# One layer with 32 experts on one core: expert groups in another order, the order of the experts computed sooner, the surplus loop moved up

## The chip, the cores and the metric

The kernel runs on one core of a Trainium2 chip. The time is the device time in microseconds (us) of one execution; less is better. Three executions of the kernel before took 603.98, 604.2 and 605.28 us, with a median of 604.2 us.

## What is computed

The reference is one layer on 256 tokens of width 1024: a norm, an input projection, a gated recurrent part beside a differential attention, an output projection with a residual, and then a mixture of 32 experts, of which each token uses two. The change touches the mixture of experts and the last norm:

```python
h2 = rmsnorm(x, norm2_g[l])
x = x + hier_moe(h2, ...)          # router, then the loop below
for e in range(N_EXPERTS):         # 32 experts, 1024 -> 512 -> 1024
    hid = jax.nn.silu(t @ w_eg[e]) * (t @ w_eu[e])
    out = out + gates[:, e:e + 1] * (hid @ w_ed[e])
return rmsnorm(x, normf_g)
```

Each expert has three float32 matrices of 2 MB, gate, up and down. All 32 are read from HBM, 201 MB in all.

## The kernel before

The first 145 us are the part ahead of the experts (projections, attention, recurrence, router). The experts follow in groups. A **pair** is two experts with room for 64 tokens each, a **four** is four experts with room for 32 tokens each, so that every group fills the 128 rows of a tile. Experts 0 to 3 are the two fixed pairs. The other 28 are sorted at run time by how many tokens they have: the fullest eight go into four pairs, the other twenty into five fours. The list `groups` has the two fixed pairs, then the four sorted pairs, then the five fours.

One group goes through these steps: one-hot matrices (`one_hot`, L838) gather its tokens (`gather`, products at L799, scaled on VectorE at L800); the gate and up products run in `up` (L877), with Silu on ScalarE in between (`gate`, L884); `hidden` multiplies (L812), transposes (L816) and copies (L819); `down` multiplies by the down matrices (L894); and `scatter` adds the result to the four sums `acc` (L832), after `halves` has split it in two parts (L825, L826). The main loop emits the preparation of group g+1 between the up and the down products of group g. A product of a pair fills half of TensorE's columns, one of a four a quarter, so two or four of them run side by side; one step in the inner dimension takes a pair or a four equally long.

The weights come through a ring of 23 buffers of 1 MB, `order`, each filled by one DMA that SyncE (SP) issues at L767. A pair needs 12 of them, a four 24. SP works in order: for each load it waits until TensorE has freed the buffer, and until the load eight places earlier on one of eight DMA semaphores (`DMAHW0` to `DMAHW7`) has landed. For the sorted experts SP first reads their numbers out of the tile `permi` (L858).

`by_load` makes the sorted order with small products and VectorE operations: a count (L918, L920), a rank (L931) and the sorted list (L936), which VectorE casts into `permi` (L937). It is a generator, and the code that calls it sets after which products each part may stand (`issue_after`). The scheduler fills in the rest.

Tokens that don't fit into their expert's room are done in a loop behind a condition on the count `nov` (`tc.If`, `tc.For_i`, L1020 and L1021). In the executions shown it is skipped. Where it is skipped, SP still has to add to the DMA semaphores what the loop's six loads would have added; it does this at the end of its own branch, one semaphore after the other, and waits before each one until all earlier loads of that semaphore have landed.

At the end (L1002 onwards) the last four's gate and up products run, then `hidden`, eight products that spread the last norm's gain over all rows (L1012, from the 4 KB that ScalarE loads at L1007), the surplus loop, four products that keep the clock up (`keep_warm(NW5, ...)`, L186), the last down products (L894), the last sums (L1094), and the norm with the stores. The buffers `nfb`, `hT_l`, `zt`, `jk` and the loop's `wx_free` are ring buffers that are asked for with `free(i)`, each a different one.

Of the kernel before, what the change touches and what calls it, by code (L numbers as in the profile page):

```python
# [29 lines left out]
FF = 512  # L30
CAP = 64
# [6 lines left out]
NWA, NWB, NWZ = 6, 11, 6  # L38
NPJ = 4
NST = 4  # L40
NWARM, NW1, NW2, NW3, NW5 = 9, 2, 10, 4, 4
NL = 3


# [3 lines left out]
B_TRI, B_ONE, B_IG, B_WR, B_RB, B_NF, B_N = 176, 304, 432, 464, 784, 824, 952  # L48

N_FIX, N_PAIRED = 4, 12  # L50
# [54 lines left out]
def kernel(ctx: ExitStack, tc: tile.TileContext,  # L105
                       x, w_in, w_out, w_eg, w_eu, w_ed, pack_a, pack_b, pack_m, out, dbg=None):
# [632 lines left out]
    def pmm():  # L739
        return psm.tile([P, 512], F32, name="pmm", tag="pmm", bufs=4)  # L740
# [4 lines left out]
    wzs.append(ctx.enter_context(tc.tile_pool(name="wzl", bufs=1, side="right", reuse_waits="tile")))  # L745
    order = [wa] + wbs[:7] + [wa] + wbs[7:9] + [wa] + wbs[9:] + [wa] + wzs[:2] + [wa] * 2 + wzs[2:]
    count, loaded = [0], [None]
    groups = [range(j, j + 2) for j in range(0, N_PAIRED, 2)] + [range(j, j + 4) for j in range(N_PAIRED, NE, 4)]
    LAST = len(groups) - 1

    def load_w(src, rows, hf, pieces):

# [38 lines left out]
    def gather(n, G_, xg=None, per=4, ks=range(KD)):  # L791

        if xg is None:
            xg = mp.tile([P, KD, P], F32, name="xg", tag="xg", bufs=1)
        for k0 in ks[::per]:
            px_ = pmm()
            for i in range(per):
                for t in range(NT):
                    T.matmul(px_[:, i * P:i * P + n], x1c[:, t, k0 + i], G_[:, t], start=(t == 0), stop=(t == NT - 1))  # L799
            V.tensor_tensor(xg[:, k0:k0 + per, :n], px_.rearrange("p (k s) -> p k s", k=4)[:, :per, :n],  # L800
                            cb[:, B_N2 + k0:B_N2 + k0 + per, None].to_broadcast([P, per, n]), op=OP.mult)
        return xg

    def free(i):

        w = order[(count[0] + i) % len(order)].tile([P, 4, 512], F32, name="w", tag="w")
        return w.rearrange("p a b -> p (a b)")

    def hidden(n, sg_, pu_, gs, to=None):
        hid = mp.tile([P, 512], F32R, name="oH", tag="oH", bufs=1).bitcast(F32).rearrange("p (k s) -> p k s", k=4)  # L810

        V.scalar_tensor_tensor(hid[:n], sg_[:n].rearrange("p (q k) -> p k q", k=4), gs[:n, :1],  # L812
                               pu_[:n].rearrange("p (q k) -> p k q", k=4), op0=OP.mult, op1=OP.mult)
        pt = pmm()
        for k in range(4):
            T.transpose(pt[:, k * P:k * P + n], hid[:n, k], ident[:n, :n])  # L816
        hT = mp.tile([P, 512], F32R, name="oL", tag="oL", bufs=1).bitcast(F32) if to is None else to
        hT = hT.rearrange("p (k s) -> p k s", k=4)
        A.copy(hT[:, :, :n], pt.rearrange("p (k s) -> p k s", k=4)[:, :, :n])  # L819
        return hT  # L820
# [21 lines left out]
    def prep(g):  # L842

        js = groups[g]
        Gm = one_hot(js).rearrange("p t e c -> p t (e c)")
        if js[0] < N_FIX:
            r = rw[:, :, g]
        elif js[0] < N_PAIRED:
            r = rw2[:, :, g - N_FIX // 2]
        else:  # L850
            r = rw4[:, :, g - N_PAIRED // 2]
        return gather(P, Gm), *slots(P, Gm, r)

    def load(g):
# [14 lines left out]
    def up(ws, n_, xg, p_=None, ks=range(KD)):  # L869
        if p_ is None:  # L870
            p_ = pgu()
        n = len(ws) // 6
        cap = P // n
        for k in ks:
            for i in range(n):
                k4 = k % 4
                up_end[0] = T.matmul(p_[i * cap:(i + 1) * cap], xg[:, k, i * cap:(i + 1) * cap],  # L877
                         ws[n_, i, k // 4][:, k4 * FF:(k4 + 1) * FF], start=(k == 0), stop=(k == KD - 1))
        return p_

    def gate(ws, xg, rs, sg_=None, p_=None):
        if sg_ is None:
            sg_ = mp.tile([P, FF], F32R, name="oL", tag="oL", bufs=1).bitcast(F32)
        A.activation(sg_, up(ws, "g", xg) if p_ is None else p_, AF.Silu, scale=rs[:, :1])  # L884
        return sg_

    def down(ws, hT, ojs):
        n = len(ws) // 6
        cap = P // n
        for k in range(4):  # L890
            for j in range(2):
                for i in range(n):
                    c0 = (k % 2) * D + j * 512
                    T.matmul(ojs[j][i * cap:(i + 1) * cap], hT[:, k, i * cap:(i + 1) * cap],  # L894
                             ws["d", i, k // 2][:, c0:c0 + 512], start=(k == 0), stop=(k == 3))
        return ojs
# [14 lines left out]
    def by_load():  # L911

        E2 = 2 * NE
        km, kc = cb[:NE, B_KM:B_KM + NE], cb[:NE, B_KC:B_KC + NE]
        kmc, kcc, ec, half = (cb[:E2, B_KC + NE + i:B_KC + NE + i + 1] for i in range(4))
        pc = pmm()
        for t in range(NT):
            T.matmul(pc[:NE, :NE], warm[:, :NE], oh[:, t], start=(t == 0), stop=(t == NT - 1))  # L918
        for t in range(NT):
            T.matmul(pc[:NE, NE:NE + 1], oh[:, t], warm[:, 0:1], start=(t == 0), stop=(t == NT - 1))  # L920
        yield
        room = mp.tile([P, 512], F32R, name="oH", tag="oH", bufs=1).bitcast(F32)[:E2]
        key, kcol, pos = room[:NE, :NE], room[:NE, NE:NE + 1], room[:, NE + 1:NE + 2]
        bef, Pe = room[:NE, E2:E2 + NE].bitcast(BF16).rearrange("p (a e) -> p a e", a=2), room[:NE, 2 * E2:2 * E2 + NE // 2].bitcast(BF16)
        V.tensor_scalar(kcol, pc[:NE, NE:NE + 1], kmc[:NE], kcc[:NE], op0=OP.mult, op1=OP.add)
        V.tensor_tensor(key, pc[:NE, :NE], km, op=OP.mult)
        V.tensor_tensor(key, key, kc, op=OP.add)

        V.tensor_scalar(bef, key[:, None, :].to_broadcast([NE, 2, NE]), kcol, None, op0=OP.is_lt)
        V.tensor_copy(cnt, pc[:NE, NE:NE + 1])  # L930
        T.matmul(pc[:E2, E2:E2 + 1], bef.rearrange("p a e -> p (a e)"), warm[:NE, 0:1], start=True, stop=True)  # L931
        yield
        V.tensor_tensor(pos, pc[:E2, E2:E2 + 1], half, op=OP.add)
        V.tensor_scalar(Pm, iota[:E2, :E2], pos, None, op0=OP.is_equal)
# [43 lines left out]
    next(positions)  # L978
    p_0 = {"g": up(ws, "g", xg, None, range(4))}
    with tc.issue_after(up_end[0].ins):  # L980
        next(positions)
        p_0["u"] = up(ws, "u", xg, None, range(4))
    with tc.issue_after(up_end[0].ins):
        next(positions)
        gather(P, Gm, xg, 2, range(4, KD))
    for n_ in "gu":
        up(ws, n_, xg, p_0[n_], range(4, KD))
# [11 lines left out]
            scatter(P, S_, oj, j)  # L999
        ws = ws_n  # L1000
    xg_l, S_l, gs_l, rs_l = pre
    sg_l = gate(ws, xg_l, rs_l, free(0)[:, :FF])  # L1002
    hT_l = free(1)[:, :512]

    nfb = free(2)
    nfr = nfb[:KD, D:D + P]
    A.dma_start(nfr, pack_b[:KD, B_NF:])  # L1007
    hT_l = hidden(P, sg_l, up(ws, "u", xg_l), gs_l, hT_l)
    for j in range(2):
        p_ = pmm()  # L1010
        for k in range(4):
            T.matmul(p_[:, k * P:(k + 1) * P], ident[:KD, 4 * j + k:4 * j + k + 1].to_broadcast([KD, P]),  # L1012
                     nfr, start=True, stop=True)
        A.copy(nfb[:, j * 512:(j + 1) * 512], p_)
    tc.keep_in_program_order(A.preload_act_table_set(SET_EXP_LN))
    wx_free = [free(i) for i in range(3, 10)]
    zt, jk = free(10), free(11)

    n_ov = nc.values_load(nov[0:1, 0:1], min_val=0, max_val=2 * S // (CAP // 2 + 1))
    with tc.If(n_ov > 0):  # L1020
        with tc.For_i(0, n_ov, 1):  # L1021
# [31 lines left out]
                    SY.dma_start(wx[n_, hf], v[:, hf * 2048:(hf + 1) * 2048])  # L1053
            Gm = mp.tile([P, NT, 2, CAP], F32, name="Gm", tag="Gm", bufs=1)[:, :, 0]
            V.tensor_tensor(Gm, iota[:, None, :].to_broadcast([P, NT, CAP]), cr.to_broadcast([P, NT, CAP]), op=OP.is_equal)
            xg = gather(CAP, Gm, wx_free[6][:, :KD * P].rearrange("p (k s) -> p k s", k=KD))
            S_, gs, rs = slots(CAP, Gm, cw)
            pg_, pu_ = pgu(), pgu()
            for n_, p_ in (("g", pg_), ("u", pu_)):
# [18 lines left out]
                scatter(CAP, S_, oj, j)  # L1078


    ss = mp.tile([P, NT, 2], F32, name="ss")
    zt = [zt[:, t * D:(t + 1) * D] for t in range(NT)]
    oj = [pgu(), pgu()]
    keep_warm(NW5, oj[1])
    down(ws, hT_l, oj)
    oH = [jk[:, j * 512:(j + 1) * 512].bitcast(F32R) for j in range(2)]
    oL = [jk[:, (2 + j) * 512:(3 + j) * 512].bitcast(F32R) for j in range(2)]
    for j in range(2):
# [72 lines left out]
```

## Time and profile before

| | |
|---|---|
| median of three executions | 604.2 us |
| profiled execution: its time, its span | 603.43 us, 601.7 us |
| TensorE busy | 534.5 us (89%) |
| loads of the experts' weights | 1024 KB each, some of the last in halves and quarters |
| moved by DMA | 223.77 MB, 372 GB/s over the span |
| chain that ended last | PE 60%, DMA 34%, DVE 2% |
| waits of SP for a ring buffer, on L877 and L894 | 93.7 us and 58.6 us |

The profile is of one execution; its span lies 1.73 us below its time, and the time 0.8 us below the median. TensorE is almost always busy until about 360 us, and from 340 us on the DMA engines are. So a reader has to go by stretches: which of the two sets the pace in which stretch, and what the other one does meanwhile.

### The profile page before, as it was taken

How to read it: one execution, taken by the hardware profiler on the slowest of the kernel's cores; microseconds unless marked ns; L12 is line 12 of the kernel's file. 1: busy time of each engine (PE TensorE's matmuls, PEld its weight loads, DVE VectorE, ACT ScalarE, POOL GpSimd, SP SyncE). 2: the span in 40 equal slices, each digit the busy share in tenths (PEclk: the TensorE clock that was granted, in tenths of full speed). 3: DMA queues.
4: the chain of work that ended last, by engine and by line, in shares of the span. 5: the costliest groups of instructions: out<-in, count | busy, mean ns of one | idle time of the engine just before them, and what ended most of it. 6: DMA issues, size and time to landing. Idle time of an engine off the chain costs nothing.

```text
span 601.7 us, 8069 instructions
## 1 busy us (share of the span) xinstructions
PE 534.5 (89%) x3039; PEld 269.6 (45%) x3039; DVE 163.5 (27%) x472; ACT 125.1 (21%) x291; POOL 9.2 (2%) x19
## 2 busy tenths in 40 slices
PE   7999999998999999999999997979777877785774
PEld 6898779795453535353535242423222222220121
DVE  4774788855131202020202001020001000100004
ACT  5675477672010000000000001000000000000023
POOL 0000003101000000000000000000000000000000
PEclk8999999999999999999999998989899988799777
DMA  8965799878599999999999999999999999999992
GB/s 301 393 193 132 238 397 364 352 281 349 205 392 422 401 423 400 412 415 387 421 384 421 383 423 419 419 421 420 422 419 420 422 419 422 420 422 420 420 394 106
DMA packets 40780, 223.77 MB, mean 372 GB/s; under 512 B 3740, under 2 KB 6180, under 8 KB 16548
## 3 DMA queue, kind: packets, MB, share of 16 engines
q1 hardware_dynamic: 40436, 222.89, 92.5%
q8 instruction: 25, 0.41, 0.3%
q10 hardware_dynamic: 304, 0.35, 0.2%
q14 instruction: 15, 0.12, 0.0%
HBM read 221.39 MB, written 1.84 MB: 371 GB/s over the span
## 4 chain that ended last, share of the span: by engine, by line
PE 60%; DMA 34%; DVE 2%; ACT 1%; issue 1%; SPq 0%; ACTq 0%
PE pmm L877 19%; DMA w<-in_w_ed_dram 13%; DMA w<-in_w_eg_dram 10%; PE pmm L894 10%; DMA w<-in_w_eu_dram 10%; PE pmm L799 5%; PE acc L832 3%; PE pj L264 3%; PE pj L261 3%; PE pj L263 3%; PE pj L274 1%; PE pj L275 1%; PE acc L612 1%; PE pj L273 1%; PE acc L613 1%; PE acc L614 1%
## 5 line engine op out<-in xcount | busy, mean ns | idle before, releaser
L877 PE MATMUL pmm<-w,xg 128*32 128x512 f32 (+1 forms) x1024 | 213.2, 634 | 29.6 <-DMA w<-in_w_eu_dram 15.0
L877 PEld LDWEIGHTS pmm<-w,xg 128*32 128x32 f32 (+1 forms) x1024 | 53.1, 125 | 158.2 <-issue 100.6
L894 PE MATMUL pmm<-w,oL 128*32 128x512 f32 (+1 forms) x448 | 87.8, 658 | 8.4 <-ACT oL L819 6.1
L894 PEld LDWEIGHTS pmm<-w,oL 128*32 128x32 f32 (+1 forms) x448 | 26.2, 130 | 62.8 <-issue 47.0
L233 DVE TENSOR_TENSOR wl<-w,wh 128x512 fp32r<-128x512 f32 (+1 forms) x72 | 44.8, 631 | 24.1 <-ACT wh L232 22.0
L826 DVE TENSOR_TENSOR oL<-pmm,oH 128x512 fp32r<-128x512 f32 x20 | 13.8, 692 | 134.3 <-PE pmm L894 91.0
L232 ACT ACTIVATE wh<-w 128x512 fp32r<-128x512 f32 (+1 forms) x72 | 41.2, 582 | 29.8 <-PE pj L263 12.5
L799 PEld LDWEIGHTS pmm<-Gm,x1c 128*128 128x128 f32 x352 | 40.8, 192 | 14.7 <-PE pmm L877 7.4
L799 PE MATMUL pmm<-Gm,x1c 128*128 128x128 f32 x352 | 44.2, 280 | 0.9 <-DVE ctr L970 0.5
L825 ACT CAST oH<-pmm 128x512 fp32r<-128x512 f32 x20 | 11.7, 586 | 121.9 <-PE pmm L894 83.4
L263 PE MATMUL pj<-hL,wh 128*128 128x256 f32 x128 | 36.6, 290 | 0.0
L261 PE MATMUL pj<-hH,wh 128*128 128x256 f32 x128 | 35.9, 292 | 0.0
L264 PE MATMUL pj<-hH,wl 128*128 128x256 f32 x128 | 35.9, 291 | 0.0
L819 ACT COPY oL<-pmm 128x512 f32<-128x512 f32 x10 | 5.9, 586 | 118.0 <-PE pmm L816 118.0
L800 DVE TENSOR_TENSOR xg<-pmm,cb 128x512 f32<-128x512 f32 (+1 forms) x24 | 15.2, 645 | 51.9 <-PE pmm L877 36.9
L884 ACT ACTIVATE oL<-pmm,rg 128x512 f32<-128x512 f32 x10 | 6.9, 688 | 103.5 <-PE acc L832 54.8
L812 DVE SCALAR_TENSOR_TENSOR oH<-oL,rg,pmm 128x512 f32<-128x512 f32 x10 | 11.3, 1127 | 55.6 <-PE pmm L877 52.6
L264 PEld LDWEIGHTS pj<-hH,wl 128*128 128x128 f32 x128 | 24.2, 193 | 1.4 <-issue 1.2
L263 PEld LDWEIGHTS pj<-hL,wh 128*128 128x128 f32 x128 | 24.7, 193 | 0.1
L261 PEld LDWEIGHTS pj<-hH,wh 128*128 128x128 f32 x128 | 24.3, 193 | 0.2
L816 PE MATMUL pmm<-ca,oH 128*128 128x128 f32 x44 | 7.9, 308 | 11.6 <-DVE oH L812 11.6
L613 PE MATMUL acc<-wh,yL 128*128 128x256 f32 (+1 forms) x48 | 15.1, 322 | 0.0
(344 smaller groups left out, 474.9 us busy)
## 6 DMA issues: line engine op xcount, KB each, us to landing
w<-in_w_eg_dram SPq DMA_DIRECT2D x64, 1024.0 KB, 12.6
w<-in_w_eu_dram SPq DMA_DIRECT2D x64, 1024.0 KB, 17.2
w<-in_w_ed_dram SPq DMA_DIRECT2D x60, 1024.0 KB, 11.0
w<-in_w_in_dram SPq DMA_DIRECT2D x10, 1024.0 KB, 14.3
w<-in_w_out_dram SPq DMA_DIRECT2D x4, 1024.0 KB, 12.5
w<-in_w_ed_dram SPq DMA_DIRECT2D x4, 512.0 KB, 17.4
w<-in_w_ed_dram SPq DMA_DIRECT2D x8, 256.0 KB, 6.7
w<-in_w_in_dram SPq DMA_DIRECT2D x3, 512.0 KB, 7.6
```

Source lines behind the costliest of these rows:

```text
L232: A.activation(wh, raw, AF.Copy)
L233: V.tensor_tensor(wl, raw, wh.bitcast(F32), op=OP.subtract)
L261: T.matmul(om, wh[:, cs], hH[:, k], start=(k == 0 and m % 2 == 0), stop=False, skip_group_check=True)
L263: T.matmul(om, wh[:, cs], hL[:, k], start=False, stop=False, skip_group_check=True)
L264: T.matmul(om, wl[:, cs], hH[:, k], start=False, stop=(k == KD - 1), skip_group_check=True)
L613: T.matmul(po[t], yL[:, k, ts], wh, start=False, stop=False, skip_group_check=True)
L799: T.matmul(px_[:, i * P:i * P + n], x1c[:, t, k0 + i], G_[:, t], start=(t == 0), stop=(t == NT - 1))
L800: V.tensor_tensor(xg[:, k0:k0 + per, :n], px_.rearrange("p (k s) -> p k s", k=4)[:, :per, :n], cb[:, B_N2 + k0:B_N2 + k0 + per, None].to_b ...
L826: V.tensor_tensor(oL[:n], oj[:n], oH[:n].bitcast(F32), op=OP.subtract)
L832: T.matmul(acc[j][t], S_[:n, t * P:(t + 1) * P], o_[:n], start=False, stop=stop, skip_group_check=True)
L877: up_end[0] = T.matmul(p_[i * cap:(i + 1) * cap], xg[:, k, i * cap:(i + 1) * cap], ws[n_, i, k // 4][:, k4 * FF:(k4 + 1) * FF], start=(k = ...
L894: T.matmul(ojs[j][i * cap:(i + 1) * cap], hT[:, k, i * cap:(i + 1) * cap], ws["d", i, k // 2][:, c0:c0 + 512], start=(k == 0), stop=(k == 3))
```

## The change

The main loop's list has the fixed pairs first and then a four and a sorted pair by turns, with a four at the end. The rank and the list of the sorted order stand among the first up products. The surplus loop stands ahead of the last up products; the last norm's gain, the last hidden and `zt` use buffers of the loop (`wx_free[:3]`) behind it. `keep_warm` has 8 and 4 products inside the last down products in place of 4 ahead of them.

```diff
-NWARM, NW1, NW2, NW3, NW5 = 9, 2, 10, 4, 4
+NWARM, NW1, NW2, NW3, NW5 = 9, 2, 10, 4, (0, 8, 4, 0)
...
-    groups = [range(j, j + 2) for j in range(0, N_PAIRED, 2)] + [range(j, j + 4) for j in range(N_PAIRED, NE, 4)]
+    pairs = [range(j, j + 2) for j in range(0, N_PAIRED, 2)]
+    fours = [range(j, j + 4) for j in range(N_PAIRED, NE, 4)]
+
+    groups, rest = pairs[:N_FIX // 2], pairs[N_FIX // 2:]
+    for i, js in enumerate(fours):
+        groups += [js] + rest[i:i + 1]
...
     with tc.issue_after(up_end[0].ins):
-        next(positions)
-        p_0["u"] = up(ws, "u", xg, None, range(4))
+        pe = next(positions)
+    with tc.issue_after(pe.ins):
+        p_0["u"] = up(ws, "u", xg, None, range(2))
     with tc.issue_after(up_end[0].ins):
-        next(positions)
+        pe = next(positions)
+    with tc.issue_after(pe.ins):
+        up(ws, "u", xg, p_0["u"], range(2, 4))
+    with tc.issue_after(up_end[0].ins):
         gather(P, Gm, xg, 2, range(4, KD))
...
-    sg_l = gate(ws, xg_l, rs_l, free(0)[:, :FF])
-    hT_l = free(1)[:, :512]
-
-    nfb = free(2)
-    nfr = nfb[:KD, D:D + P]
-    A.dma_start(nfr, pack_b[:KD, B_NF:])
-    hT_l = hidden(P, sg_l, up(ws, "u", xg_l), gs_l, hT_l)
...
-    wx_free = [free(i) for i in range(3, 10)]
-    zt, jk = free(10), free(11)
+    room = free(0)
+    sg_l = gate(ws, xg_l, rs_l, room[:, :FF])
+    wx_free = [free(i) for i in range(1, 7)]
...
     with tc.If(n_ov > 0):
...
+    nfb, zt, hT_l = wx_free[:3]
+
+    nfr = nfb[:KD, D:D + P]
+    A.dma_start(nfr, pack_b[:KD, B_NF:])
+    hT_l = hidden(P, sg_l, up(ws, "u", xg_l), gs_l, hT_l[:, :512])
...
+    jk = free(7)
     oj = [pgu(), pgu()]
-    keep_warm(NW5, oj[1])
-    down(ws, hT_l, oj)
+    warm_to = pgu()
+    for k, n in enumerate(NW5):
+        down(ws, hT_l, oj, (k,))
+        if n:
+            keep_warm(n, warm_to)
```

The first place is TensorE (PE) at the first group, about 147 to 158 us in the trace. Before, with the rank product at L931 and the list product at L936:

```order
L920 MATMUL pmm<-warm,oh 32x1
L877 MATMUL pmm<-w,xg 64x512 x15
L931 LDWEIGHTS oH
L931 MATMUL pmm<-warm,oH 64x1
L877 MATMUL pmm<-w,xg 64x512
L799 MATMUL pmm<-Gm,x1c 128x128 x4
L936 LDWEIGHTS warm
L936 MATMUL pmm<-oH,warm 128x32
L799 MATMUL pmm<-Gm,x1c 128x128 x4
```

and now, with the same two products at L937 and L941:

```order
L926 MATMUL pmm<-warm,oh 32x1
L883 MATMUL pmm<-w,xg 64x512 x8
L937 LDWEIGHTS oH
L937 MATMUL pmm<-warm,oH 64x1
L883 MATMUL pmm<-w,xg 64x512 x4
L941 LDWEIGHTS warm
L941 MATMUL pmm<-oH,warm 128x32
L883 MATMUL pmm<-w,xg 64x512 x4
L805 MATMUL pmm<-Gm,x1c 128x128 x8
```

The list product has 12 expert products ahead of it instead of 16 and four gather products.

The second place is PE at the second group, where the third is prepared. Before, the third group is a pair (`rw` with 3 columns, products of 64 rows):

```order
L877 MATMUL pmm<-w,xg 64x512 x5
L799 MATMUL pmm<-Gm,x1c 128x128 x16
L779 MATMUL pmm<-ca,Gm 128x128 x2
L781 MATMUL pmm<-rw_1865,Gm 128x3 x2
L816 MATMUL pmm<-ca,oH 128x128 x4
L894 MATMUL pmm<-w,oL 64x512 x16
L877 MATMUL pmm<-w,xg 64x512 x11
```

and now it is a four (5 columns, products of 32 rows):

```order
L883 MATMUL pmm<-w,xg 64x512 x5
L805 MATMUL pmm<-Gm,x1c 128x128 x16
L785 MATMUL pmm<-ca,Gm 128x128 x2
L787 MATMUL pmm<-rw_1866,Gm 128x5 x2
L822 MATMUL pmm<-ca,oH 128x128 x4
L900 MATMUL pmm<-w,oL 64x512 x16
L883 MATMUL pmm<-w,xg 32x512 x13
```

From here on fours and pairs alternate.

The third place is ScalarE (ACT) at the end, with what each instruction waits for. Before, the 4 KB load, the Silu, the copy of the hidden and the two copies of the gain all stand ahead of the condition on `nov`:

```order
L1007 DMA w<-in_pack_b_dram 8x128 [waits DMAHW4_49,DMAHW3_49,DMAHW5_49,DMAHW2_49,DMAHW6_49,DMAHW1_49,DMAHW7_49,DMAHW0_49,PE_49]
L884 ACTIVATE w<-pmm,rg 128x512 [waits DMAHW7_49,DMAHW0_49,PE_49]
L819 COPY w<-pmm 128x512 [waits DMAHW0_49,PE_49]
L1014 COPY w<-pmm 128x512 [waits PE_49] x2
L1015 ACT_TABLE_LOAD
L1019 TENSOR_LOAD nov [waits DVE_49]
L1020 COMPARE_AND_BRANCH
```

and now the load and the three copies stand behind the skipped loop (L1017 is ACT's own branch):

```order
L1017 UNCONDITIONAL_BRANCH [waits Activation_49]
L1081 DMA w<-in_pack_b_dram 8x128 [waits DMAHW3_49,DMAHW4_49,DMAHW2_49,DMAHW5_49,DMAHW1_49,DMAHW6_49,DMAHW0_49,PE_49]
L825 COPY w<-pmm 128x512 [waits DMAHW3_49,DMAHW4_49,DMAHW2_49,DMAHW5_49,DMAHW0_49,PE_49]
L1088 COPY w<-pmm 128x512 [waits PE_49] x2
L1101 CAST w<-pmm 128x512 [waits PE_49] x2
L1110 ACTIVATE xg,ss<-acc_1395 128x512 [waits PE_49]
```

The value of `DMAHW6` that L1081 waits for is 464. All loads of that semaphore together bring it to 448; the missing 16 are those that SP adds where it skips the loop. In the kernel before, none of ACT's waits at this place is on such a value. SP's end of the skipped loop (L1017, with its waits) stands behind its last load and ahead of the stores:

```order
L1050 DMA w<-in_w_ed_dram 128x2048 [waits DMAHW3_49,PE_49]
L1018 REGISTER_ALU
L1018 COMPARE_AND_BRANCH
L1018 UNCONDITIONAL_BRANCH [waits DMAHW1_49,DMAHW0_49,DMAHW2_49,SP_sequencer_49,DMAHW3_49,DVE_sequencer_49,DMAHW4_49,PE_sequencer_49,DMAHW5_49,Activation_sequencer_49,DMAHW6_49,Pool_sequencer_49,DMAHW7_49,DVE_49,Pool_49,PE_49,Activation
L1017 UNCONDITIONAL_BRANCH [waits SP_sequencer_49,DMAHW0_49,DMAHW1_49,DMAHW2_49,DMAHW3_49,DMAHW6_49,DMAHW7_49]
L1128 DMA out_dram<-w 128x512 [waits DMAHW7_49,DVE_49]
```

There SP goes through the semaphores in the order of the last but one row. What it awaits of `DMAHW3` is the load two places before the very last.

## Rows read from the trace of the kernel before

**Rows 1.** Page, the span in 40 equal slices: what the DMA engines moved.

```profile
GB/s 301 393 193 132 238 397 364 352 281 349 205 392 422 401 423 400 412 415 387 421 384 421 383 423 419 419 421 420 422 419 420 422 419 422 420 422 420 420 394 106
```

**Rows 2.** Busy time by stage: us (count) per engine, PEclk, DMA share, GB/s.

```profile
150.00:160.00 10.00, 9.60 (x48) 4.23 (x46) 1.67 (x7) 0.00 (x0) 0.00 (x0) 1.00 0.34 107
...
180.00:340.00 160.00, 156.63 (x761) 64.84 (x758) 26.10 (x54) 12.82 (x21) 0.00 (x0) 1.00 0.99 406
340.00:580.00 240.00, 191.46 (x1099) 65.48 (x1100) 21.43 (x45) 13.21 (x22) 0.00 (x0) 0.91 1.01 420
```

**Rows 3.** Chain that ended last, one pair: start us, us, what.

```profile
211.32 5.14 PE pmm L877 x22
...
235.50 7.09 PE pmm L894 x32
242.59 5.14 PE pmm L877 x22
```

**Rows 4.** Busy time by pair (columns as in 2), first and last of the four sorted pairs.

```profile
211.30:242.60 31.30, 30.63 (x150) 12.81 (x146) 4.81 (x9) 2.45 (x4) 0.00 (x0) 1.00 0.99 406
...
305.10:336.40 31.30, 30.63 (x152) 12.60 (x152) 5.11 (x11) 2.45 (x4) 0.00 (x0) 1.00 0.99 403
```

**Rows 5.** Timeline at the sorted order: start us, us, engine, instruction.

```profile
147.47 7.08 PE L877 MATMUL pmm<-w,xg 128*64 128x512 f32 x30
...
154.48 0.19 PE L931 MATMUL pmm<-warm,oH 32*64 32x1 bf16 x1
...
156.69 0.18 PE L936 MATMUL pmm<-oH,warm 32*128 32x32 bf16 x1
...
157.14 0.18 DVE L937 CAST permi<-pmm 128x32 int32<-128x32 f32 x1
...
158.99 0.94 SPq L767 DMA_DIRECT2D w<-in_w_eg_dram  x2
```

**Rows 6.** Timeline of TensorE: warm products, gain products, the last down products.

```profile
140.37 2.33 PE L189 MATMUL pm<-warm 128*128 128x512 bf16 x10
...
576.71 2.26 PE L1012 MATMUL pmm<-w,ca 8*128 8x128 f32 x16 [1.38 <-DMA w<-in_pack_b_dram]
...
579.79 1.87 PE L186 MATMUL pmm<-warm 128*128 128x512 bf16 x4 [0.82 <-ACTq L1020]
...
589.83 0.14 PEld L894 LDWEIGHTS pmm<-w 128*32 128x32 f32 x2 [0.33 <-DMA w<-in_w_ed_dram]
```

**Rows 7.** Chain that ended last, the end: start us, us, what.

```profile
572.13 4.45 DMA w<-in_pack_b_dram
...
581.66 9.22 PE pmm L894 x64
590.88 1.92 PE acc L1094 x7
```

**Rows 8.** Line L858, SP reads the experts' numbers: duration ns min/median/max.

```profile
L858 SPq TENSOR_LOAD <-permi x28: 262/264/472, 157.3 to 178.3; - x28
```

**Rows 9.** Timeline of ScalarE at the end, idle time and releaser in brackets.

```profile
572.79 0.69 ACT L884 ACTIVATE w<-pmm,rg 128x512 f32<-128x512 f32 x1 [38.87 <-DMA w<-in_pack_b_dram]
575.37 0.59 ACT L819 COPY w<-pmm 128x512 f32<-128x512 f32 x1 [1.90 <-DMA w<-in_w_ed_dram]
```

**Rows 10.** Timeline of SP, the last two loads: start us, us, engine, instruction.

```profile
584.60 0.86 SPq L767 DMA_DIRECT2D w<-in_w_ed_dram  x2
```

**Rows 11.** Line L1020 on SP, the skipped loop: duration ns min/median/max, first to last.

```profile
L1020 SPq EVENT_SEMAPHORE  x7: 17/17/17, 585.7 to 588.6; - x7
```

**Rows 12.** DMA issues from ScalarE: KB each, us from issue to landing.

```profile
out_dram<-w ACTq DMA_DIRECT2D x1, 256.0 KB, 2.7
```

**Rows 13.** TensorE at the end in stretches: us, busy (count), PEclk, DMA share, GB/s.

```profile
578.00:580.00 2.00, 1.18 (x8) 0.59 1.03 399
...
582.00:584.00 2.00, 2.00 (x12) 0.50 1.02 383
584.00:586.00 2.00, 2.00 (x20) 0.71 0.96 338
```

More of the change, by code (lines that the diff above doesn't have):

```diff
@@ L747 @@
     count, loaded = [0], [None]
-    groups = [range(j, j + 2) for j in range(0, N_PAIRED, 2)] + [range(j, j + 4) for j in range(N_PAIRED, NE, 4)]
+    pairs = [range(j, j + 2) for j in range(0, N_PAIRED, 2)]
[3 more added lines that the diff above has]
+        groups += [js] + rest[i:i + 1]
     LAST = len(groups) - 1
+    assert sum(map(len, groups)) == NE and len(groups[LAST]) == 4
     def load_w(src, rows, hf, pieces):
@@ L846, in prep @@
         if js[0] < N_FIX:
-            r = rw[:, :, g]
+            r = rw[:, :, js[0] // 2]
         elif js[0] < N_PAIRED:
-            r = rw2[:, :, g - N_FIX // 2]
+            r = rw2[:, :, (js[0] - N_FIX) // 2]
         else:
-            r = rw4[:, :, g - N_PAIRED // 2]
+            r = rw4[:, :, (js[0] - N_PAIRED) // 4]
         return gather(P, Gm), *slots(P, Gm, r)
@@ L885, in gate, with down @@
         return sg_
-    def down(ws, hT, ojs):
+    def down(ws, hT, ojs, ks=range(4)):
         n = len(ws) // 6
         cap = P // n
-        for k in range(4):
+        for k in ks:
             for j in range(2):
@@ L930, in by_load @@
         V.tensor_copy(cnt, pc[:NE, NE:NE + 1])
-        T.matmul(pc[:E2, E2:E2 + 1], bef.rearrange("p a e -> p (a e)"), warm[:NE, 0:1], start=True, stop=True)
-        yield
+        yield T.matmul(pc[:E2, E2:E2 + 1], bef.rearrange("p a e -> p (a e)"), warm[:NE, 0:1], start=True, stop=True)
         V.tensor_tensor(pos, pc[:E2, E2:E2 + 1], half, op=OP.add)
@@ L935, in by_load @@
         V.tensor_scalar(Pe, Pm[:NE, :NE], ec[:NE], None, op0=OP.mult)
-        T.matmul(pc[:, 3 * NE:4 * NE], warm[:NE], Pe, start=True, stop=True)
+        pe = T.matmul(pc[:, 3 * NE:4 * NE], warm[:NE], Pe, start=True, stop=True)
         V.tensor_copy(permi, pc[:, 3 * NE:4 * NE])
         V.tensor_copy(permf, pc[:, 3 * NE:4 * NE])
-        yield
+        yield pe
     def in_order():
@@ L1001 @@
     xg_l, S_l, gs_l, rs_l = pre
-    sg_l = gate(ws, xg_l, rs_l, free(0)[:, :FF])
-    hT_l = free(1)[:, :512]
-    nfb = free(2)
-    nfr = nfb[:KD, D:D + P]
-    A.dma_start(nfr, pack_b[:KD, B_NF:])
-    hT_l = hidden(P, sg_l, up(ws, "u", xg_l), gs_l, hT_l)
[L1009 to L1014, printed above, removed]
+    room = free(0)
+    sg_l = gate(ws, xg_l, rs_l, room[:, :FF])
+    wx_free = [free(i) for i in range(1, 7)]
     tc.keep_in_program_order(A.preload_act_table_set(SET_EXP_LN))
-    wx_free = [free(i) for i in range(3, 10)]
-    zt, jk = free(10), free(11)
     n_ov = nc.values_load(nov[0:1, 0:1], min_val=0, max_val=2 * S // (CAP // 2 + 1))
@@ L1055 @@
             V.tensor_tensor(Gm, iota[:, None, :].to_broadcast([P, NT, CAP]), cr.to_broadcast([P, NT, CAP]), op=OP.is_equal)
-            xg = gather(CAP, Gm, wx_free[6][:, :KD * P].rearrange("p (k s) -> p k s", k=KD))
+            xg = gather(CAP, Gm, room[:, FF:FF + KD * P].rearrange("p (k s) -> p k s", k=KD))
             S_, gs, rs = slots(CAP, Gm, cw)
@@ L1078 @@
                 scatter(CAP, S_, oj, j)
+    nfb, zt, hT_l = wx_free[:3]
+    nfr = nfb[:KD, D:D + P]
+    A.dma_start(nfr, pack_b[:KD, B_NF:])
+    hT_l = hidden(P, sg_l, up(ws, "u", xg_l), gs_l, hT_l[:, :512])
+    for j in range(2):
+        p_ = pmm()
+        for k in range(4):
+            T.matmul(p_[:, k * P:(k + 1) * P], ident[:KD, 4 * j + k:4 * j + k + 1].to_broadcast([KD, P]),
+                     nfr, start=True, stop=True)
+        A.copy(nfb[:, j * 512:(j + 1) * 512], p_)
     ss = mp.tile([P, NT, 2], F32, name="ss")
     zt = [zt[:, t * D:(t + 1) * D] for t in range(NT)]
+    jk = free(7)
     oj = [pgu(), pgu()]
-    keep_warm(NW5, oj[1])
-    down(ws, hT_l, oj)
+    warm_to = pgu()
[3 more added lines that the diff above has]
+            keep_warm(n, warm_to)
     oH = [jk[:, j * 512:(j + 1) * 512].bitcast(F32R) for j in range(2)]
```

## The prediction

> **What bounds the kernel now.** I read the page's slices first, then busy time by stage, then the chain of waits for one pair and for the end, then the timelines of the engines at the two places where the chain changes hands.
>
> The slices [rows 1] show the DMA engines at 419 to 423 GB/s in the last third, but at 400, 412, 415, 387 and 384 in slices of the middle. The stages [rows 2] say why. From 340 to 580 us they move 420 GB/s while TensorE is busy for 191 of 240 us: DMA sets the pace. From 180 to 340 us they move 406 GB/s while TensorE is busy for 156.6 of 160 us: there TensorE sets it. Those are mainly the four sorted pairs. Each takes 31.27 us, from one start of its gate products to the next (242.59 - 211.32) [rows 3], with TensorE busy for 30.63 us of it and DMA at 403 to 406 GB/s [rows 4]. Its 12 loads of 1.0486 MB would take 12.58 MB / 420 GB/s = 29.96 us. So a pair costs the DMA stream 1.3 us, and four pairs 5.2 us.
>
> The other hole is at 150 to 160 us with 107 GB/s [rows 2]. There SP has no numbers for the sorted experts: the list product runs at 156.69, the cast into `permi` at 157.14, the first two sorted loads at 158.99 [rows 5].
>
> At the end the last piece of weights lands at about 589.8 us, since the last weight load of TensorE, at 589.83, was waiting for it [rows 6]. I call this moment L. The last down products end at 590.88 [rows 7], 1.1 us later; the last sums, norm and stores take the remaining 11 us and are not changed. So the time is L + 1.1 + 11, and the change can gain only by an earlier L, and lose only behind it.
>
> **The change part by part: an earlier L.** Three edits bear on it.
>
> The list product gets 12 expert products ahead of it in place of 16 and four gather products. In pairs 12 products are 6 steps; 30 products and weight loads took 7.08 us from 147.47 on [rows 5], so 15 products or some 8 steps, 0.88 us each, 5.3 us for six. 147.47 + 5.3 = 152.8 in place of 156.69: 3.9 us sooner. Against this, the first sorted group is now a four, so SP reads four numbers and not two before its first load. One read takes 0.26 us [rows 8]; from the cast to the first load, with two reads and their arithmetic, 1.67 us passed (157.32 to 158.99) [rows 5], so two more cost between 0.5 and 1.7; I take 1.2. This leaves 2.7 us. Not all of it becomes an earlier L: the buffers of the fixed pairs come free at TensorE's old pace, and SP waits for them next. Between 0 and 2.7 I take 1.5.
>
> Fours and pairs by turns: a pair and a four are 36 loads, 37.75 MB, 89.9 us at 420 GB/s. TensorE needs 30.6 us for the pair [rows 4]. For a four: 240 us at 420 GB/s are 96 loads, four fours, for which it was busy for 191.46 us [rows 2], or 47.9 each, part of them at the lower clock. The sum, 78.5, is 11 us less than the DMA's time, and the 23 buffers let the loads of one group run while TensorE is still at the one before. So the pairs no longer throttle, and 4 x 1.3 = 5.2 us come back; with the whole stretch of 180 to 340 us, 160 x (1 - 406/420) = 5.3, the bounds are 3 (some pair is still waited for) and 5.7.
>
> Together L comes 6.7 us sooner, between 3 and 8.4.
>
> **What comes behind L.** Before, ScalarE issued the 4 KB load of the gain at 572.13, the Silu of the last group ran at 572.79, and the copy of the last hidden at 575.37, all ahead of the condition [rows 7, 9], so that the last down products took the pieces as they landed. Now the load, the copy and the gain's copies stand behind the skipped loop, as the third place of the order shows, in buffers that the loop has also used. The load waits for `DMAHW6` at 464. The loads alone bring 448. The last 16 come from SP in its branch for the skipped loop, and SP adds there one semaphore after the other, each after its own loads: `DMAHW3`, ahead of `DMAHW6`, awaits the load two places before the very last. Before, SP issued its last two loads at 584.60 to 585.46 [rows 10] and went through these additions from 585.7 to 588.6 [rows 11], so it ended 1.2 us before L. The new loop stands at the same place in SP's row, behind all loads. So ScalarE can issue the 4 KB no earlier than about L - 1.2.
>
> What is queued behind it: on ScalarE the copy of the hidden and the gain's copies, and on TensorE, in its order, the gain products (which read the 4 KB), then every one of the last down products. Before, the copy of the hidden, which follows the last up products, ran at 575.37 [rows 9], L - 14.4; TensorE comes to that point at the same distance from L and then idles for some 16 us, until L + 1.5, while the weights of the last downs lie there unused.
>
> The terms from L on:
> - Issue at L - 1.2, landing 2.7 us later, as for the only other late load or store of ScalarE in the list of issues [rows 12]: L + 1.5. Bounds: the copy of the hidden alone decides, L + 0.1; or as crowded as before, 4.45 us [rows 7], L + 3.3.
> - Gain products 2.26 us [rows 6].
> - The down products of a four are eight rounds of four side by side, those of a pair eight rounds of two: 7.09 us in the full clock [rows 3].
> - 12 warm products within them, at 0.233 us (ten in 2.33) [rows 6]: 2.8 us. Before, four lay under TensorE's wait; these twelve lie under nothing.
> - The clock. Before, the granted clock fell to 0.59 in the stretch of 578 to 580, after gaps between TensorE's groups of work; it stayed at 0.50 (1.2 GHz) and was back at 1 in that of 584 to 586 (0.71) [rows 13]. With work from 579.79 on [rows 6] that is 5.4 us at half speed, to 585.2, worth 2.7 us; 0.3 us of it is already in the gain products' 2.26. I take +2.4. Bounds: none, or from 578.4 to 585.2, 6.8 us, worth 3.1.
>
> Sum: 1.5 + 2.3 + 7.1 + 2.8 + 2.4 = L + 16.1 in place of L + 1.1: 15.0 us later. Bounds: 0.1 + 12.2 - 1.1 = 11.2, and 3.3 + 12.2 + 3.1 - 1.1 = 17.5.
>
> The row for the landing says 2.7 us on an idle queue and 4.45 beside the stream. The Trainium skill ("DMA: Bandwidth & Descriptors", "Rules for kernel authors") advises to issue a DMA early and wait for it late, so that its fixed cost is covered; it speaks against this change, which issues as late as can be and waits at once. The same page ("Anatomy of one DMA — SWDGE (gpsimd) path") puts the fixed cost at about 2.0 us, on another issue path; by that, as an estimate, the sum would be 0.7 us less.
>
> Net: 15.0 - 6.7 = 8.3 us more. On the profiled execution, 603.43 + 8.3 = 611.7; the median of the three runs lies 0.8 us above that execution, so 612. Own range: 11.2 - 8.4 = +2.8 and 17.5 - 3 = +14.5, that is 607 to 619.
>
> **Rivals.**
> 1. The hold isn't there or is released early: the 4 KB load goes out more than some 8 us before L, lands under the stream, and the last downs follow the pieces as before. Then only the gain is left: 603.4 - 6.7 + 0.8 = 597.5, faster. For it: before, ScalarE's load was held too (Silu idle for 38.87 us behind it [rows 9]) and still came out at L - 18, so a wait that looks long need not be last. Against: that wait was on loads that land early; this one is on a value that no load brings. Chance 0.06.
> 2. The clock stays at half through all of the last downs, since TensorE has stood for longer than before: 12.2 us of work become 24.4, L + 1.5 + 24.4 - 0.3 = L + 25.6, net 24.5 - 6.7 = +17.8, 622. For it: a longer gap; against: in [rows 13] it rose while such products ran. Chance 0.08.
> 3. The gain does not come: the pair between two fours is throttled still, since the loads of a four fill the ring and its buffers come free late, or the reads of numbers cost what the earlier order gives. With 1 us of gain, 15.0 - 1 = +14.0: 618. For it: TensorE is busy nearly throughout until 340 us [rows 2]; against: the 11 us of slack. Chance 0.10.
>
> **How the numbers follow.** My forecast has 0.76, the rivals 0.06, 0.08 and 0.10. 0.2% of the time, 1.2 us, is about what a measurement of this kernel can tell from no change. Faster is rival 1: 0.06. Between it and the forecast lies a release some 8 to 9 us earlier than I think, which would cancel the gain: 0.02 for no change, taken from the forecast. The rest, 0.92, is slower. For 8 in 10 the range leaves out rivals 1 and 2 and takes 607 to 619, with one us more below, as the three runs of before lie 1.3 us apart: 606 to 619.
>
> **What would show it.** In the changed kernel's profile: the first sorted load at about 156 us; 420 GB/s in the slices from some 215 us on, without the 384s; the last landing at about 583; ScalarE's 4 KB load issued after SP's last load, about a us ahead of that landing, with the skipped loop as what it waited for; TensorE idle for some 16 us ahead of the gain products and at 0.5 of its clock when it starts; the last down products ending some 16 us behind the last landing; a span of about 610. I am wrong if the 4 KB load goes out ahead of SP's last loads (then rival 1), if TensorE's clock is 0.5 throughout the last downs (rival 2), or if the last landing stays near 589 (rival 3).

## The result, and the profile after

The changed kernel took 613.69 us (median of four; 612.33 to 615.4) beside 604.74 us for the kernel before. The ratio is 1.0148, with a 95% interval of 1.0115 to 1.018: it is slower by 9 us. The profiled execution took 614.13 us with a span of 612.3 us, 10.7 and 10.6 us above that of before.

First the part that gains. The page's slices of what the DMA engines moved, which answer to [rows 1]:

```profile
GB/s 290 393 190 130 277 366 339 381 248 333 317 394 419 383 422 421 421 420 419 422 420 421 420 422 420 421 419 421 420 423 420 421 420 420 422 419 420 390 27 70
```

From the fifteenth slice on, 214 us into the span, nothing is under 419 until the loads end (390); before, the dips to 387, 384 and 383 went on until 346 us. By stage, with the columns of [rows 2]:

```profile
150.00:160.00 10.00, 10.00 (x54) 4.23 (x52) 1.76 (x7) 0.00 (x0) 0.00 (x0) 1.00 0.53 170
...
180.00:340.00 160.00, 152.00 (x887) 62.68 (x884) 23.27 (x54) 11.33 (x19) 0.00 (x0) 1.00 1.01 416
340.00:570.00 230.00, 190.54 (x951) 66.87 (x949) 22.70 (x44) 13.49 (x21) 0.00 (x0) 0.94 1.01 421
```

416 GB/s in place of 406 from 180 to 340 us, and TensorE now has idle time there (152.0 of 160 us busy, before 156.6). SP's waits name the same thing (line, what was waited for: us in total, times, longest):

```profile
SPq L773 <- PE pmm L883: 22.9, 22, 4.5
...
SPq L773 <- PE pmm L900: 15.4, 10, 8.6
```

Before, these two were 93.7 and 58.6 us: the buffers that TensorE frees are seldom what the loads wait for now. At the sorted order (timeline, as in [rows 5], with the ten warm products ahead of the experts, as in [rows 6]):

```profile
141.17 2.33 PE L189 MATMUL pm<-warm 128*128 128x512 bf16 x10
...
154.02 0.18 PE L941 MATMUL pmm<-oH,warm 32*128 32x32 bf16 x1
...
154.24 0.19 DVE L942 CAST permi<-pmm 128x32 int32<-128x32 f32 x1 [1.29 <-PE pmm L941]
...
157.24 1.51 SPq L773 DMA_DIRECT2D w<-in_w_eg_dram  x3
```

By the clocks of the two traces the list product is 2.7 us sooner (154.02 for 156.69) and SP's first sorted load 1.75 us (157.24 for 158.99). But this execution came to the experts 0.8 us later: the ten warm products start at 141.17 us, before at 140.37, and no edit touches what stands ahead of them. Counted from these products, the list product is 3.5 us sooner and the first sorted load 2.55 us.

Now the end. SP's additions for the skipped loop (the line's seven instructions, first to last, as in [rows 11]), SP's own timeline, and the timeline of all engines there:

```profile
L1017 SPq EVENT_SEMAPHORE  x7: 17/17/17, 580.4 to 583.9; - x7
```

```profile
574.73 5.45 SPq L773 DMA_DIRECT2D w<-in_w_ed_dram  x5
```

```profile
571.94 0.66 PE L822 MATMUL pmm<-ca,oH 128*128 128x128 f32 x4 [1.26 <-DVE oH L818]
583.94 0.54 ACTq L1081 DMA_DIRECT2D w<-in_pack_b_dram  x1
584.73 0.59 ACT L825 COPY w<-pmm 128x512 f32<-128x512 f32 x1 [34.24 <-DMA w<-in_w_ed_dram]
...
585.62 3.75 PE L1086 MATMUL pmm<-w,ca 8*128 8x128 f32 x16 [13.03 <-DMA w<-in_pack_b_dram]
```

The five loads that end at 574.73 + 5.45 = 580.18 are SP's last; before, SP was at that point at 585.46 [rows 10]. So SP is 5.3 us ahead, and 6.1 us when both are counted from the warm products. The last piece landed at 589.83 before. Now nothing waits for it, so it has no row of its own; the trace's record of its semaphore, `DMAHW5`, is complete at 585.05. That is 4.8 us sooner, or 5.6 us counted from the warm products. TensorE does the last hidden's transposes at 571.94, and then nothing for 13.0 us. ScalarE issues the 4 KB load at 583.94, right behind the last of SP's additions at 583.9, and only then comes its copy of the hidden (584.73). The chain of waits that ended last (start us, us, what) has what follows:

```profile
583.94 1.55 DMA w<-in_pack_b_dram
585.49 0.14 issue
585.62 3.75 PE pmm L1086 x16
589.37 5.53 PE pmm L900 x32
594.90 1.83 PE pmm L186 x8
596.73 1.85 PE pmm L900 x16
598.59 0.97 PE pmm L186 x4
599.55 1.85 PE pmm L900 x16
```

It ends at 601.41, 16.4 us behind the last landing. The stretches of TensorE (columns as in [rows 13]) show at which clock:

```profile
574.00:576.00 2.00, 0.00 (x0) 1.00 1.02 401
576.00:578.00 2.00, 0.00 (x0) 0.56 1.04 396
...
590.00:592.00 2.00, 2.00 (x16) 0.50 0.00 0
592.00:594.00 2.00, 2.00 (x20) 0.67 0.00 0
594.00:596.00 2.00, 2.00 (x18) 1.00 0.00 0
```

The clock goes to 0.50 while TensorE stands idle and is back in 592 to 594; the gain products take 3.75 us in place of 2.26 [rows 6], the first half of the downs 5.53 us, the second half 2 x 1.85.

### The profile page after: what moved, and what is told of

It reads as the page before. It is cut to its first block, busy times and chain, and to the rows that moved or that the text cites. A ratio compares the mean times of both kernels' runs of the same rounds, so it can differ in the third digit from the quotient of the medians.

```text
span 612.3 us, 8091 instructions
## 1 busy us (share of the span) xinstructions
PE 535.2 (87%) x3047; PEld 273.0 (45%) x3047; DVE 163.4 (27%) x472; ACT 125.0 (20%) x291; POOL 9.0 (1%) x19
## 5 line engine op out<-in xcount | busy, mean ns | idle before, releaser
L883 PE MATMUL pmm<-w,xg 128*32 128x512 f32 (+1 forms) x1024 | 200.9, 610 | 19.2 <-DMA w<-in_w_eu_dram 13.8
L900 PE MATMUL pmm<-w,oL 128*32 128x512 f32 (+1 forms) x448 | 98.2, 637 | 12.0 <-ACT oL L825 6.1
L900 PEld LDWEIGHTS pmm<-w,oL 128*32 128x32 f32 (+1 forms) x448 | 28.7, 129 | 74.1 <-issue 47.2
L832 DVE TENSOR_TENSOR oL<-pmm,oH 128x512 fp32r<-128x512 f32 x20 | 13.8, 692 | 132.8 <-PE pmm L900 106.7
L805 PEld LDWEIGHTS pmm<-Gm,x1c 128*128 128x128 f32 x352 | 40.8, 192 | 15.2 <-issue 7.7
L822 PEld LDWEIGHTS pmm<-ca,oH 128*128 128x128 f32 x44 | 5.2, 153 | 22.9 <-issue 20.2
```

Of the source, the lines that this page charges most:

```text
L832: V.tensor_tensor(oL[:n], oj[:n], oH[:n].bitcast(F32), op=OP.subtract)
```

## The experiments

Theory A: the 4 KB load is held because it adds to a DMA semaphore (`DMAHW6`) to which the loop's loads add as well. It must be preceded by all of those, and where the loop is skipped that is SP's addition, behind SP's last load. Theory B, closer to the words of my prediction: it is held because it writes a buffer that the loop uses. Each kernel was run beside the kernel before, on the same chip.

**e1, buffers of their own.** What isn't shared with the loop any more is nfb, zt and the last hidden (jk, which wasn't shared, moves to another number):

```diff
-    nfb, zt, hT_l = wx_free[:3]
+    nfb = free(7)
...
-    hT_l = hidden(P, sg_l, up(ws, "u", xg_l), gs_l, hT_l[:, :512])
+    pu_l = up(ws, "u", xg_l)
+    hT_l = hidden(P, sg_l, pu_l, gs_l, free(8)[:, :512])
...
-    jk = free(7)
+    zt, jk = free(9), free(10)
```

> The changed kernel, but nfb, zt, the last hidden and jk get ring buffers of their own (numbers 7 to 10) that the surplus loop never uses; the 4 KB load still stands behind the loop. Theory A (what holds the 4 KB load is the DMA semaphore that it shares with the loop's loads, DMAHW6 at 464, whatever buffer it writes): no change from the changed kernel, about 613.5 us, TensorE idle for 13 us ahead of the gain products as there. Theory B (the shared buffers hold it, as my prediction put it): the last down products take the pieces as they land, about 599.5 us (604.7 minus the 5.3 us by which SP's last load went out sooner).

Measured: 613.51 us, ratio 1.0145 (1.0121 to 1.0169), the same as the changed kernel. ScalarE's row for the load has lost its other waits and kept one DMA semaphore:

```
L1080 DMA w<-in_pack_b_dram 8x128 [waits DMAHW6_49,PE_49]
```

The value is 464 as before, and the load itself adds 16 to it. SP's line and the timeline:

```profile
L1017 SPq EVENT_SEMAPHORE  x7: 17/17/17, 579.5 to 583.0; - x7
```

```profile
571.47 0.66 PE L822 MATMUL pmm<-ca,oH 128*128 128x128 f32 x4 [1.26 <-DVE oH L818]
583.06 0.54 ACTq L1080 DMA_DIRECT2D w<-in_pack_b_dram  x1
...
584.66 3.75 PE L1086 MATMUL pmm<-w,ca 8*128 8x128 f32 x16 [12.54 <-DMA w<-in_pack_b_dram]
```

The load goes out at 583.06, behind SP's last additions (the last at 583.0), and the gain products follow at 584.66. The copy of the hidden no longer waits for the loop's additions; it stood behind the load on ScalarE all the same. Theory A stands, and theory B falls as the only reason. In the changed kernel the loop's own load of that buffer adds to `DMAHW6` as well, so the buffer too would ask for 464 there; without the buffer the wait is the same.

**e2, the load ahead of the loop.** It writes a free corner of `room`, and the rest stays in the loop's buffers:

```diff
     room = free(0)
+    nfr = room[:KD, FF + KD * P:FF + KD * P + P]
+    A.dma_start(nfr, pack_b[:KD, B_NF:])
...
-    nfr = nfb[:KD, D:D + P]
-    A.dma_start(nfr, pack_b[:KD, B_NF:])
```

> The changed kernel, but the 4 KB load stands ahead of the surplus loop and writes a free corner of the buffer `room`; the last hidden, zt and nfb stay in the loop's buffers. The copy of the last hidden now waits for DMAHW1 at 480, SP's second addition. Theory A: the copy comes after that addition, at about 582.5 on the changed kernel's clock, the gain products are done by then, and the last down products start at about 583.2 in place of 589.4, still at half clock at first: 4 to 5 us less than the changed kernel, about 609 us. Theory B (only the load mattered, the copy is free): about 599.5. Rival (the load was no part of the hold, the copy alone was): about 613.

Measured: 606.86 us, ratio 1.0041 (1.0023 to 1.0058). 6.7 us less than e1, where I had expected 4 to 5.

```profile
L1019 SPq EVENT_SEMAPHORE  x7: 17/17/17, 579.9 to 582.8; - x7
```

```profile
566.35 0.53 ACTq L1013 DMA_DIRECT2D w<-in_pack_b_dram  x1
...
571.03 3.32 PE L1086 MATMUL pmm<-w,ca 8*128 8x128 f32 x16 [1.30 <-DMA w<-in_pack_b_dram]
580.84 0.59 ACT L825 COPY w<-pmm 128x512 f32<-128x512 f32 x1 [11.93 <-DMA w<-in_w_ed_dram]
...
581.48 5.44 PE L900 MATMUL pmm<-w 128*32 128x512 f32 x32 [7.14 <-ACT w L825]
```

The load goes out at 566.35 and the gain products run at 571.03, under the stream. The copy of the hidden (580.84) comes between SP's first addition (579.9) and its last (582.8): here the shared buffer is what holds it, by its wait for `DMAHW1` at 480. The downs start at 581.48 and not at 583.2, since the loads of `DMAHW1` had landed sooner than I had put it (complete at 580.74 in this trace, at 582.42 in that of the changed kernel). So there are two holds, one behind the other: the load's semaphore, and the buffer of the hidden.

**e3, both.** The two edits together; the loop is still ahead of the last up products.

> Both edits at once: the 4 KB load ahead of the loop in `room`, and buffers of their own for nfb, zt, the last hidden and jk. The loop stays ahead of the last up products. Theories A and B: nothing is left that waits for SP's additions, the last down products follow the pieces, end some 1 to 2 us behind the last landing: 604.7 - 5.3 = about 599.5 us (599 to 601, the twelve warm products may cost up to 1). Rival (the place of the loop itself, or the warm products, cost the 15 us): over 608.

Measured: 598.84 us, ratio 0.9921 (0.9897 to 0.9945). Once nothing behind it waits for SP's additions, the place of the loop no longer costs the 15 us; whether it costs anything, e9 shows.

```profile
571.47 0.59 ACT L825 COPY w<-pmm 128x512 f32<-128x512 f32 x1 [2.76 <-PE pmm L822]
...
573.34 4.15 PE L900 MATMUL pmm<-w 128*32 128x512 f32 x32
...
582.08 3.09 PE L900 MATMUL pmm<-w 128*32 128x512 f32 x16
...
584.12 0.14 PEld L900 LDWEIGHTS pmm<-w 128*32 128x32 f32 x2 [0.50 <-DMA w<-in_w_ed_dram]
```

The downs start at 573.34, and their last weights are loaded at 584.12, when the last piece has landed; they end 1 us later, as before.

**e4, TensorE kept awake.** 56 warm products in the idle 13 us:

```diff
-    hT_l = hidden(P, sg_l, up(ws, "u", xg_l), gs_l, hT_l[:, :512])
+    hT_l = hidden(P, sg_l, up(ws, "u", xg_l), gs_l, hT_l[:, :512])
+    keep_warm(56, pgu())
```

> The changed kernel with 56 more warm products (bf16, 512 columns, 0.233 us each at full clock, some 13 us) between the last hidden's transposes and the gain products, where TensorE stands idle for 13 us. If the half clock at the restart (0.50 from 576 to 593 in the changed kernel's stretches) comes from the idle time, the gain products take 2.2 in place of 3.75 us and the first half of the downs 3.6 in place of 5.5: 3.5 us less, about 610 us. If the clock falls for another reason, no change, 613.5; if the warm products outlast the hold, up to 1 us more than that.

Measured: 610.06 us, ratio 1.0104 (1.0078 to 1.013), 3.6 us less than the changed kernel.

```profile
571.84 12.25 PE L186 MATMUL pmm<-warm 128*128 128x512 bf16 x56
583.84 0.54 ACTq L1081 DMA_DIRECT2D w<-in_pack_b_dram  x1
...
585.41 2.05 PE L1087 MATMUL pmm<-w,ca 8*128 8x128 f32 x16 [1.32 <-DMA w<-in_pack_b_dram]
...
587.38 3.64 PE L900 MATMUL pmm<-w 128*32 128x512 f32 x32
```

```profile
578.00:580.00 2.00, 2.00 (x11) 1.00 0.98 354
...
586.00:588.00 2.00, 2.00 (x22) 1.00 0.03 8
```

The clock stays at 1.00, the gain products take 2.05 us and the first half of the downs 3.64. The low clock at the restart came from the idle time; its price is 3.6 us.

**e5 and e6, the two gains alone.** e5 is the kernel before with the new `groups` (and the tables of weights indexed by `js[0]`); e6 the kernel before with `by_load`'s parts among `up(..., range(2))` and `up(..., range(2, 4))`, both as in the diff of the change.

> The kernel before with only the order of the groups changed (fours and pairs by turns). My theory: the four sorted pairs no longer throttle the stream, 420 GB/s from some 215 us on; the last load goes out 3.5 us sooner, less the two more numbers that SP reads ahead of the first sorted load (0.5 to 1.2 us): about 601.2 us (600 to 602). Rival (the pairs' loss only moves elsewhere, or the gain was all due to the earlier list): 604.7, no change.

> The kernel before with only the small products of the sorted order moved in between the first gate and up products. My theory: the first sorted load goes out 2.7 us sooner (1.75 in the changed kernel, which reads two more numbers), but the pairs that follow are at TensorE's pace, so little of it reaches the end: 604.0 us (603 to 604.7). Rival (each us sooner there is a us sooner at the end): 602.

Measured: e5 599.97 us, ratio 0.9916 (0.9891 to 0.994), 4.7 us faster; e6 603.55 us, ratio 0.9974 (0.9956 to 0.9991), 1.2 us faster. The slices of the two, e5 first:

```profile
GB/s 281 394 211 116 228 409 349 321 304 345 146 423 404 421 403 421 420 421 419 420 422 420 420 420 420 421 420 421 420 422 421 420 419 422 421 422 420 420 386 111
```

```profile
GB/s 288 393 210 132 252 392 358 367 268 350 288 380 407 393 409 395 424 392 410 418 389 422 382 420 422 420 420 421 419 422 420 422 418 422 420 423 418 422 389 104
```

e5 is at 419 to 422 from the sixteenth slice on; e6 still has 392, 389 and 382 there. In e5 SP's first sorted load comes late (timelines of TensorE and of SP):

```profile
142.57 2.33 PE L189 MATMUL pm<-warm 128*128 128x512 bf16 x10
...
162.49 7.84 SPq L771 DMA_DIRECT2D w<-in_w_eg_dram  x7
```

By the clock that is 3.5 us behind the kernel before, but 2.2 us of it are there ahead of the experts already (142.57 for 140.37). Counted from the warm products the two reads cost 1.3 us, close to the 1.2 that I had charged. It gains all the same: the place where the list comes is worth little, that of the pairs much. In e6 (the same two timelines) the first sorted load is 4.5 us sooner by the clock and 3.7 us counted from the warm products:

```profile
139.54 2.33 PE L189 MATMUL pm<-warm 128*128 128x512 bf16 x10
...
154.47 9.66 SPq L767 DMA_DIRECT2D w<-in_w_eg_dram  x4
```

**e7, the end alone.** The kernel before with the changed kernel's end.

> The kernel before with only the end changed: the surplus loop ahead of the last up products, the 4 KB load, nfb, zt and the last hidden behind it in the loop's buffers, and the warm products within the last downs. My theory: the whole price of the tail without any gain, 604.7 + 15.8 = about 620.5 us (619 to 622). Rival (the tail is held only because the last load comes sooner): less than 616.

Measured: 619.6 us, ratio 1.0244 (1.0216 to 1.0271): 14.9 us for the tail alone, my 15.0.

**e8, without the twelve warm products.** `NW5` is (0, 0, 0, 0) in the changed kernel.

> The changed kernel without the twelve warm products within the last downs. By my sum they lie on the path at full clock: 2.8 us less, about 610.9 us. Rival (they cover a wait or keep the clock up): no change, 613.5, or longer downs after them.

Measured: 611.3 us, ratio 1.0097 (1.0068 to 1.0126), 2.4 us less. The downs are one run now:

```profile
590.29 9.04 PE L900 MATMUL pmm<-w 128*32 128x512 f32 x64
```

9.04 us, as much as their parts in the changed kernel (5.53 + 2 x 1.85 = 9.23): the warm products neither hid anything nor sped anything up.

**e9, both gains with the old end**; e10, e3 without the warm products; e11, e3 with the list sooner:

```diff
-    p_0 = {"g": up(ws, "g", xg, None, range(4))}
+    p_0 = {"g": up(ws, "g", xg, None, range(2))}
...
     with tc.issue_after(pe.ins):
-        p_0["u"] = up(ws, "u", xg, None, range(2))
+        up(ws, "g", xg, p_0["g"], range(2, 3))
...
     with tc.issue_after(pe.ins):
-        up(ws, "u", xg, p_0["u"], range(2, 4))
+        up(ws, "g", xg, p_0["g"], range(3, 4))
+        p_0["u"] = up(ws, "u", xg, None, range(4))
```

> The kernel before with the new order of the groups and the sorted order's products among the first gate and up products, but with the old end (loop behind the last up products, four warm products ahead of the downs). If the gains add up, 604.7 - 4.7 (groups alone) - 1.2 (order alone) = 598.8 us; and if the place of the loop is worth nothing once nothing waits for it, no difference from the kernel with the load ahead and own buffers (598.8). Rival (the new place of the loop helps by itself): 600 or more here.

> The kernel with the 4 KB load ahead of the loop and own buffers, without the twelve warm products within the last downs. There the downs end about 1 us behind the last landing, so the warm products lie under a wait: no change, 598.8 us. Rival 1 (they are on the path): about 1 us less. Rival 2 (they keep the clock up): TensorE at 0.5 in the last stretches and up to 2 us more.

> The kernel with the 4 KB load ahead of the loop and own buffers, with the rank product after 2 and the list product after 3 of the first gate products' steps, so that SP's first sorted load goes out some 2.7 us sooner (154.6 in place of 157.3). As the order's products alone brought 1.2 us for a first load 4.5 us sooner, about 0.3 us for each: 598.1 us. Rival 1 (each us counts at the end): 596.1. Rival 2 (SP waits for the fixed pairs' buffers next): no change, 598.8.

Measured: e9 597.22 us, ratio 0.9882 (0.9865 to 0.9899), the fastest median of all and 7 us faster than before; e10 598.08 us, 0.99 (0.9883 to 0.9916); e11 597.91 us, 0.988 (0.9862 to 0.9897). The intervals of the three overlap, so none is shown to beat the others, and e10's can't be told from e3's either. For e9 and e3 the intervals just overlap at their ends. The traces, one of each kernel, say more when they are counted from the ten warm products:

| us | warm products start | from there to the first sorted load | to the end of SP's last load | to the end of the span |
|---|---|---|---|---|
| before | 140.37 | 18.6 | 445.1 | 461.3 |
| changed kernel | 141.17 | 16.1 | 439.0 | 471.1 |
| e5, groups alone | 142.57 | 19.9 | 440.8 | 457.0 |
| e6, order alone | 139.54 | 14.9 | 444.1 | 460.3 |
| e9, both, old end | 140.24 | 16.1 | 439.0 | 455.2 |
| e3, load ahead, own buffers | 140.67 | 16.1 | 439.1 | 455.4 |
| e11, e3 with the list sooner | 142.57 | 13.8 | 439.1 | 457.5 |

Behind the warm products e3 and e9 take the same time within 0.2 us, so these two traces show no worth in the old place of the loop. The groups bring SP's last load 4.3 us forward, the order alone 1.0 us, and both 6.1 us. In e11 (timelines of TensorE and of SP):

```profile
142.57 2.33 PE L189 MATMUL pm<-warm 128*128 128x512 bf16 x10
...
156.33 12.95 SPq L773 DMA_DIRECT2D w<-in_w_eg_dram  x7
```

Its first sorted load goes out 2.3 us sooner than in e3, most of the 2.7 us that the list should give, and SP's last load ends where e3's does: a still sooner list gains the stream nothing. That this trace of e11 ends 2 us later than that of e3 lies behind the stream, in TensorE's last work (granted clock 0.77 from 570 to 602 us, in e3 0.91).

## Why the prediction was right

The forecast, 612 us and slower, was met by 613.69. Its terms:

| term | predicted | measured |
|---|---|---|
| stream earlier at its end | 6.7 us | 5.6 at the last landing, 6.1 at SP's last load (traces, from the warm products on); medians 5.9 (e5 + e6), 7.0 (e9) |
| 4 KB load's issue, from the last landing | -1.2 | -1.1 (583.94 - 585.05) |
| its landing | 2.7 | 1.55 |
| gain products and downs at full clock | 9.4 | 9.3 (e4's chain: 2.05 + 3.57 + 2 x 1.85) |
| clock | +2.4 | +3.7 (12.98 - 9.32), e4 3.6 |
| twelve warm products | 2.8 | 2.8, e8 2.4 |
| end, from the last landing | +16.1 | +16.4 |
| the tail's price | 15.0 | 15.3 (trace), 14.9 (e7) |

The hold was where I had read it, in the wait for a value that no load brings, and it set the end. That the sum behind the last landing came out so close is in part luck: the landing was put 1.15 us too long and the clock 1.3 us too cheap, and the two cancel. The spans differ by 10.6 us where I had 8.3: 1.1 us is the stream, 0.3 us the tail, and 0.8 us isn't of the change but the later start of the experts in this execution. Points on which the working was off, each by no more than some 2 us:

- The cause of the hold. I put the load's wait down to the buffers "that the loop has also used". e1 shows that the buffer isn't needed for it: the load's own semaphore is enough. For the hidden the buffer is the cause (e2). Whoever had followed my words and given the buffers back would have gained nothing.
- The clock. I took the stretch of low clock from before, 5.4 us from the first product on; it lasted from the restart at 585.6 into 592 to 594, some 7.7 us. The last up products had run at half clock too (5.91 us for 3.62, from 564.77 on), so the transposes came at 571.94, 13.1 us ahead of the last landing (before at 574.68, 15.2 us ahead), and the idle time was 13 us, not 16; the end follows SP's additions, so neither moved it.
- The landing. 1.55 us for 4 KB while the stream's last pieces were landing, below the 2.7 of the 256 KB store that I had for the nearest row. The Trainium skill's 2.0 us ("DMA: Bandwidth & Descriptors", "Anatomy of one DMA — SWDGE (gpsimd) path"), for another issue path, lay closer, and above it too. Its rule to issue early and wait late ("Rules for kernel authors") is borne out by e2, where the same load lies under the stream.
- The reorder. The pairs' 5.2 us were about right (e5: 4.7, with a first sorted load 1.3 us later), and that the earlier list is worth little too (e6: 1.2, I had taken 1.5). Counted from the warm products, the list product came 3.5 us sooner and the first sorted load 2.55 us, for 3.9 and 2.7 in the working.

Rival 1, a release early enough to leave only the gain, is what e3 and e9 look like (598.8 and 597.2; it had 597.5): the price of it was right, the condition wasn't met. Rival 2 (half clock throughout) is refuted by the stretches, rival 3 (no gain) by the slices.

## What to carry to other kernels

Before work is moved behind a conditional region that is usually skipped, look at what its instructions wait for with their values: a skipped branch still adds to every semaphore that the region counts on, in one engine's order and behind that engine's earlier work, and a DMA behind it can wait for that through its own semaphore, whatever buffer it writes. Groups that are bound by different engines are better alternated than put in rows, as long as the buffers between them hold as much as the two differ by (here 23 were enough; fewer weren't tried). The price of a late start is the whole stage behind it, with the engine's clock gone down in the meantime.

## What the runs showed that was not expected

How soon the first sorted load goes out counts for little at the end: 3.7 us sooner than before gave 1.0 us in the trace (e6), with the groups alternated 3.9 us gave 1.8 (e9 beside e5), and the next 2.3 us gave nothing (e11 beside e3). With 23 buffers of work queued, the hole in the stream at 150 us is largely made up behind it. The stretch ahead of the experts, which no edit touches, differed by 4 us between traces (its warm products start at 138.54 in e10, at 142.57 in e5 and e11): two traces of this kernel are to be compared from a point that lies just ahead of the change, and not by their clocks. And 56 products that compute nothing made the changed kernel 3.6 us faster, since they kept the granted clock at 1.00 through 13 us without other work.
